# A two-block transformer on one core: six of the convolution's 31 taps become ScalarE products that DMAs add up, and its normalisation is put in another order

## The chip, the core and the metric

The kernel runs on one core of a Trainium2 chip. The metric is the device time of one execution in microseconds (us), as the median of several runs. An engine executes its own instructions strictly in the order of the program, so an instruction that waits holds up everything behind it on its engine.

## What is computed

Two transformer blocks in fp32 on 256 tokens of width 2048. The change lies in the first block, whose mixer has 16 attention heads (64 wide, three branches) beside a convolution branch with 1024 channels:

```
proj = rms_norm(x) @ w_in            # q | kv | gates | conv_in
a, gate = split(conv_in)
u = a * sigmoid(gate)                # 256 tokens x 1024 channels
u = causal_depthwise_conv(u, conv_w, conv_b)    # 31 taps
u = layer_norm(u, ln_g, ln_b)        # mean and variance over the 1024 channels
conv = silu(u)
x = x + concat([attn, conv]) @ w_out
```

After it come the block's feed-forward part and the second block, which the change does not touch.

## The kernel before, in words

The program is one list of weight items. An item is 128x1024 weights (512 KB): SyncE loads it (`raw`), ScalarE rounds it to `hi` (L281), VectorE subtracts to get `lo` (L282), and TensorE does 12 products of 128x512 with it (L164). Each of `hi` and `lo` has four buffers, so that ScalarE's cast for item n+3 can start when TensorE has finished item n-1. Eight items make a group of 512 columns. The order of the groups in the first block is the list `ORDER`: three quarters of the convolution's input (c0, c1, c2), gates, q0, cmp, c3 (the last quarter), win, slc, q1, and then the output projection, whose first part `oc` multiplies the convolution's eight blocks of 128 channels and needs no attention. Items are named here by group and place: q1.0 to q1.7, then oc.0 and so on.

Everything else is put between the items: after each half of an item the function `pump` lets each of three queues of small steps go on by a rate, the attention (`attn`), the convolution (`conv`, rates in `RATES`) and the urgent one (turning a group's result, and the like). When an item needs a convolution block that is not there, `Acts.get` runs the convolution's steps until it is.

A quarter q of the convolution has 256 channels in a 128x512 tile (two blocks side by side). One step of the queue is one tap: two VectorE instructions (L526) that multiply the shifted input `u` by a column and add to `y`; tap 30 is a ScalarE instruction with the bias (L523). When all four quarters are done, `conv_norm` goes on step by step: `mean` (TensorE with a matrix of 1/1024, over eight blocks), `center` for each quarter (VectorE subtracts, ScalarE squares), `var` (TensorE), `rs` and `rs2` (one over the root of the variance, spread over the partitions as `lnr`), then for each quarter `scale` for two halves (VectorE times `lnr`, ScalarE tanh, ScalarE gain and bias), `silu` (VectorE, then a ScalarE cast `sh`) and `low` (VectorE, `sl`). `sh` and `sl` are what oc multiplies.

At the end of q1 its result is taken from PSUM by two ScalarE copies (`e`, L428); TensorE turns `e` (L391) after oc.0, ahead of oc.1.

Of the kernel before, what the change touches and what calls it, by code (L numbers as in the profile page):

```python
# [19 lines left out]
AF = mybir.ActivationFunctionType  # L20
ALU = mybir.AluOpType
# [4 lines left out]
P = 128  # L26
T = 256
# [7 lines left out]
NU = 63  # L35
AHEAD = 3
NRAW = 4
LN_DVE = 0
ORDER = ["c0", "c1", "c2", "g", "q0", "cmp", "c3", "win", "slc", "q1", "oc", "oa", "ob"]
RATES = {"c1": {"conv": 1}, "win": {"attn": 0.25}, "q1": {"attn": 0.34, "conv": 1.5},  # L40
         "oc": {"attn": 0.5, "conv": 2}, "oa": {"attn": 1}}


# [31 lines left out]
class Pipe:  # L75


    def __init__(self):
        self.q = deque()
        self.later = []  # L80
# [26 lines left out]
class Acts:  # L107


    def __init__(self, pipe):  # L110
        self.d = {}
        self.pipe = pipe if callable(pipe) else lambda kt: pipe

    def get(self, kt):
        while kt not in self.d:
            assert self.pipe(kt).busy()
            self.pipe(kt).step()
        return self.d[kt]

    def put(self, kt, hi, lo):  # L120
# [3 lines left out]
def body(tc, A, out, stop=None, dbg=None):  # L124
# [18 lines left out]
    act, dve, pe, pool_e = nc.scalar, nc.vector, nc.tensor, nc.gpsimd  # L143
# [3 lines left out]
    def nm(s):  # L147
        cnt[0] += 1
        return f"{s}{cnt[0]}"

    def U(s="u", dt=F32):
        return big.tile([P, 512], dt, name=nm(s), tag="U", bufs=NU)

    def two(t):
        return t.rearrange("p (a b) -> p a b", a=2)

    def small(s="s"):
        return sml.tile([P, 16], F32, name=nm(s), tag="sm")

    def bank(s="bg"):  # L160
        return psB.tile([P, 512], F32, name=nm(s), tag="bg")

    def mm(o, l, r, start=False, stop=False):
        pe.matmul(o, l, r, start=start, stop=stop, skip_group_check=True)  # L164
# [138 lines left out]
    avg = keep.tile([P, P], F32, name="avg")  # L303
# [32 lines left out]
    def col(name, i):  # L336
        c = offs[name] + i
        return cols[:, c:c + 1]
# [73 lines left out]
    def turn_plain(dst, src, c0, c1=None):  # L412
        act.copy(dst, turn4(src, c0, c1))
# [72 lines left out]
    w_in = w2d("w_in")  # L486


    us, ys = {}, {}
    conv, attn = Pipe(), Pipe()  # L490
    mixT = Acts(lambda kt: conv if kt >= 8 else attn)

    def conv_in(q):

        def post(acc):
            s, u = U("sig"), U("ut")
            uu = [two(u)[:, 0], two(u)[:, 1]]
            for t in range(2):
                act.activation(two(s)[:, t], acc[t][:, :T], AF.Sigmoid, scale=rstd[:, t:t + 1])
                dve.scalar_tensor_tensor(uu[t], acc[t][:, T:], rstd[:, t:t + 1], two(s)[:, t],  # L500
                                         op0=ALU.mult, op1=ALU.mult)

            def f():
                us[q], ys[q] = U("u"), U("y")
                turn_plain(us[q], uu, 0)
                for k in range(30, -1, -1):
                    conv.push(lambda k=k: conv_tap(q, k))
                if q == 3:
                    conv_norm()
            urgent.push(None)  # L510
            urgent.push(f)
        return post

    def conv_group(q):
        group(w_in, None, 512, allk, xT, conv_in(q), parts=[(3632 + q * T, T), (2608 + q * T, T)])

    def conv_tap(q, k):
        u2, y2 = two(us[q]), two(ys[q])
        for kk in range(2):
            f = 2 * q + kk  # L520
            w = col("conv_w", k * 8 + f)
            if k == 30:
                act.activation(y2[:, kk], u2[:, kk], AF.Identity, scale=w, bias=col("conv_b", f))  # L523
            else:
                s = 30 - k
                dve.scalar_tensor_tensor(y2[:, kk, s:], u2[:, kk, :T - s], w, y2[:, kk, s:],  # L526
                                         op0=ALU.mult, op1=ALU.add)

    def conv_norm():
        st = {}  # L530

        def mean():
            b = st["m"] = bank("mean")
            for f in range(8):
                mm(b[:, :T], avg, two(ys[f // 2])[:, f % 2], start=f == 0, stop=f == 7)

        def center(q):
            mb = st["m"][:, :T].unsqueeze(1).broadcast_to([P, 2, T])
            dve.tensor_tensor(two(ys[q]), two(ys[q]), mb, op=ALU.subtract)
            s = st[q] = U("sqc")  # L540
            act.activation(s, ys[q], AF.Square)

        def var():

            b = st["v"] = bank("var")
            for t in range(2):
                for f in range(8):
                    mm(b[:, t:t + 1], two(st[f // 2])[:, f % 2, t * P:(t + 1) * P], avg[:, 0:1],
                       start=f == t == 0, stop=f == 7)

        half_gb = keep.tile([P, 16], F32, name="half_gb")

        def rs():
            c = offs["conv_ln_g"]
            dve.tensor_scalar(half_gb, cols[:, c:c + 16], 0.5, None, op0=ALU.mult)
            v = small("lnv")
            dve.tensor_scalar(v[:, :2], st.pop("v")[:, :2], EPS, None, op0=ALU.add)
            newton_rstd(v[:, 2:4], v[:, :2], 2)
            d = st["d"] = U("lnd")
            for t in range(2):  # L560
                dve.tensor_scalar(d[:, t * P:(t + 1) * P], ident, v[:, 2 + t:3 + t], 1024.0,
                                  op0=ALU.mult, op1=ALU.mult)

        def rs2():

            b = bank("lnr")
            mm(b[:, :T], avg, st.pop("d")[:, :T], start=True, stop=True)
            r = U("lnr")
            act.copy(r[:, :T], b[:, :T])
            st["r"] = r[:, :T]  # L570

        def scale(q, kk):
            y = two(ys[q])[:, kk]
            dve.tensor_tensor(y, y, st["r"], op=ALU.mult)

            if kk == 0:
                st[q] = U("th")
            f = 2 * q + kk
            g, b = half_gb[:, f:f + 1], half_gb[:, 8 + f:9 + f]
            act.activation(two(st[q])[:, kk], y, AF.Tanh, scale=g, bias=b)  # L580
            if LN_DVE:
                dve.tensor_scalar(y, y, g, b, op0=ALU.mult, op1=ALU.add)
            else:
                act.activation(y, y, AF.Identity, scale=g, bias=b)

        def silu(q):
            y = ys[q]
            dve.scalar_tensor_tensor(y, st.pop(q), 1.0, y, op0=ALU.add, op1=ALU.mult)
            hi = st["hi", q] = U("sh", F32R)
            act.copy(hi, y)  # L590

        def low(q):
            hi, lo = st["hi", q], U("sl", F32R)
            dve.tensor_tensor(lo, ys[q], hi.bitcast(F32), op=ALU.subtract)  # L594
            for kk in range(2):
                mixT.put(8 + 2 * q + kk, two(hi)[:, kk], two(lo)[:, kk])

        for f in (mean, None):
            conv.push(f)
        for q in range(4):  # L600
            conv.push(lambda q=q: center(q))
        for f in (None, var, rs, None, rs2):
            conv.push(f)
        for q in range(4):
            conv.push(lambda q=q: scale(q, 0))
            conv.push(lambda q=q: scale(q, 1), None, lambda q=q: silu(q), None, lambda q=q: low(q))

# [39 lines left out]
    def post_cmp(acc):  # L647
        e = take(acc, rstd)
        st = {}
# [22 lines left out]
        def hidden(i):  # L672
            def f():
                b = st[("b", i)] = bank("hid")
                o = b[0:64, :60]
                for lp in range(16):
                    e_, m = divmod(lp, 8)
                    xv = st[i][e_].rearrange("p (h n b) -> p h n b", h=4, b=8)
                    w = w1t[i][e_].rearrange("p (l c) -> p l c", l=8)[:, m]
                    mm(o, w, xv[:, :, e_:e_ + 15, m], start=lp == 0, stop=lp == 15)  # L680
            return f

        def silu():
            hk_ = st["hk"] = U("hidk")
            act.activation(hk_[0:64, :60], st.pop(("b", 0))[0:64, :60], AF.Silu)
            hv = st["hv"] = U("hidv")
            pool_e.memset(hv[0:64], 0.0)
            h4 = hv.rearrange("p (h g n) -> p h g n", h=4, g=4)
            src = st.pop(("b", 1))[0:64, :60].rearrange("p (h n) -> p h n", h=4)
            for g in range(4):  # L690
                act.activation(h4[0:64, :, g, 0:15], src, AF.Silu)
# [27 lines left out]
        for f in (gather(0), gather(1), hidden(0), hidden(1), silu, None, outk, outv):  # L719
            urgent.push(f)  # L720
# [261 lines left out]
    for name in ORDER:  # L982
        i0 = len(items)

        def bef(name=name):
            rates.update(RATES.get(name, {}))
            if name == "q0":
                load_M(0)
# [616 lines left out]
```

## Time and profile before

| what | value |
|---|---|
| median of 3 runs | 2831.16 us (2830.11 to 2831.34) |
| the profiled execution, its own time | 2829.45 us |
| its span, first to last instruction | 2827.5 us |
| TensorE (PE) busy | 2793.4 us, 99% |
| VectorE (DVE) busy | 1631.5 us, 58% |
| ScalarE (ACT) busy | 1423.6 us, 50% |
| GpSimd (POOL) busy | 36.6 us, 1% |
| mean granted TensorE clock | 0.996 |

Times in rows are microseconds from the start of the span; a duration runs from the start to the end of one instruction, and instructions of one engine overlap a little, so that the next one can start before the one in front has ended. Idle time in square brackets is that of the engine ahead of the row, with what ended it.

### The profile page before, as it was taken

The numbers are of one execution on the slowest core, as the hardware profiler recorded it, in microseconds if no ns is written. First come the engines' busy times: TensorE is split into PE (matmuls) and PEld (weight loads), VectorE is DVE, ScalarE is ACT, GpSimd is POOL, SyncE is SP. The second block draws the span as 40 slices with busy tenths as digits, with TensorE's granted clock in tenths as the row PEclk, the third lists the DMA queues.
The fourth block names the chain that finished last, engine by engine and source line by source line (L and its number), as shares of the span: only waits on it lengthen the run. The fifth ranks groups of instructions, "written<-read, shape, count | busy, mean of one in ns | idle before, by whom it ended". The sixth has DMA issues, their size and how long they took to land.

```text
span 2827.5 us, 34906 instructions
## 1 busy us (share of the span) xinstructions
PE 2793.4 (99%) x13031; PEld 2314.5 (82%) x13031; DVE 1631.5 (58%) x2472; ACT 1423.6 (50%) x2072; POOL 36.6 (1%) x73
## 2 busy tenths in 40 slices
PE   8998999999999999999999999999999999999998
PEld 7886778888888888889888888888888888888887
DVE  6887765656666554565554545555555455454444
ACT  5456565555555444566544555554454444444443
POOL 1200000000000000000000000000000000000000
PEclk9999999999999999999999999999999999999999
DMA  7853345666556666654566555665566666666664
GB/s 232 236 165 119 116 136 184 187 186 186 180 180 195 198 197 193 179 173 129 170 197 193 172 165 173 179 197 187 183 189 187 192 187 192 187 187 196 197 197 160
DMA packets 279579, 513.01 MB, mean 181 GB/s; under 512 B 21223, under 2 KB 46739, under 8 KB 279409
## 3 DMA queue, kind: packets, MB, share of 16 engines
q1 hardware_dynamic: 272256, 502.86, 58.4%
q0 software_dynamic: 4624, 7.13, 0.9%
q8 instruction: 102, 1.67, 0.2%
q10 hardware_dynamic: 2528, 0.79, 0.1%
q14 instruction: 69, 0.56, 0.1%
HBM read 505.45 MB, written 5.24 MB: 181 GB/s over the span
## 4 chain that ended last, share of the span: by engine, by line
PE 96%; DVE 1%; ACT 1%; issue 1%; DMA 0%; SPq 0%; DVEq 0%; ACTq 0%
PE acc L164 90%; PE tr L391 2%; PE ms L164 1%; PE o L164 0%; DMA raw<-in_w_in 0%; PE ds L164 0%; PE mo L164 0%; PE do L164 0%; DVE lo L282 0%; ACT hi L281 0%; ACT p L802 0%; PE hid L164 0%; PE s L164 0%; PE pt L807 0%; DVE y L526 0%
## 5 line engine op out<-in xcount | busy, mean ns | idle before, releaser
L282 DVE TENSOR_TENSOR lo<-raw,hi 128x1024 fp32r<-128x1024 f32 (+3 forms) x956 | 1153.3, 1211 | 1013.7 <-ACT hi L281 993.1
L281 ACT CAST hi<-raw 128x1024 fp32r<-128x1024 f32 (+3 forms) x956 | 989.8, 1040 | 879.3 <-PE acc L164 821.2
L164 PE MATMUL acc<-hi,xh 128*128 128x512 f32 (+2 forms) x3200 | 1261.2, 394 | 2.8 <-ACT xh L405 2.8
L164 PE MATMUL acc<-hi,xl 128*128 128x512 f32 (+2 forms) x3200 | 1241.8, 388 | 0.5 <-DVE xl L407 0.5
L164 PE MATMUL acc<-lo,xh 128*128 128x512 f32 (+2 forms) x3200 | 1240.0, 388 | 0.0
L164 PEld LDWEIGHTS acc<-hi,xl 128*128 128x128 f32 x3200 | 601.7, 188 | 123.7 <-DVE xl L407 1.0
L164 PEld LDWEIGHTS acc<-hi,xh 128*128 128x128 f32 x3200 | 602.2, 188 | 118.4 <-ACT xh L405 3.0
L164 PEld LDWEIGHTS acc<-lo,xh 128*128 128x128 f32 x3200 | 602.8, 188 | 115.9 <-DVE lo L282 0.5
L164 PE MATMUL acc<-hi,sh 128*128 128x512 f32 x480 | 192.1, 400 | 10.7 <-ACT sh L590 10.7
L164 PE MATMUL acc<-hi,sl 128*128 128x512 f32 x480 | 187.7, 391 | 0.0
L164 PE MATMUL acc<-lo,sh 128*128 128x512 f32 x480 | 187.6, 391 | 0.0
L164 PEld LDWEIGHTS acc<-hi,sh 128*128 128x128 f32 x480 | 90.6, 189 | 29.4 <-ACT sh L590 11.1
L164 PEld LDWEIGHTS acc<-hi,sl 128*128 128x128 f32 x480 | 90.5, 188 | 19.6 <-DVE sl L594 0.2
L164 PEld LDWEIGHTS acc<-lo,sh 128*128 128x128 f32 x480 | 90.7, 189 | 17.6
L526 DVE SCALAR_TENSOR_TENSOR y<-u,cols,y 128x255 f32<-128x255 f32 (+14 forms) x240 | 96.3, 464 | 0.0
L1043 DVE SCALAR_TENSOR_TENSOR yf<-tr,cols,yf 128x254 f32<-128x254 f32 (+1 forms) x176 | 72.6, 475 | 29.3 <-ACT yf L1038 29.3
L1038 ACT ACTIVATE yf<-tr,cols 128x256 f32<-128x256 f32 x88 | 44.8, 560 | 33.7 <-PE tr L391 33.7
L164 PE MATMUL acc<-hi,ymh 128*128 128x512 f32 x128 | 49.8, 389 | 0.0
L164 PE MATMUL acc<-lo,ymh 128*128 128x512 f32 x128 | 49.8, 389 | 0.0
L164 PE MATMUL acc<-hi,yml 128*128 128x512 f32 x128 | 49.8, 389 | 0.0
L428 ACT ACTIVATE e<-acc,rstd 128x512 f32<-128x512 f32 x54 | 37.0, 690 | 25.2 <-PE acc L164 25.2
L434 ACT ACTIVATE junk<-xs 128x512 f32<-128x512 f32 x48 | 30.0, 629 | 35.8 <-DVE xs L442 14.3
(314 smaller groups left out, 1373.5 us busy)
## 6 DMA issues: line engine op xcount, KB each, us to landing
raw<-in_w_in SPq DMA_DIRECT2D x216, 512.0 KB, 3.7
raw<-in_w_up SPq DMA_DIRECT2D x176, 512.0 KB, 3.8
raw<-in_w_down SPq DMA_DIRECT2D x88, 512.0 KB, 4.4
raw<-in_w_ffn_gate SPq DMA_DIRECT2D x88, 512.0 KB, 4.3
raw<-in_w_ffn_up SPq DMA_DIRECT2D x88, 512.0 KB, 3.8
raw<-in_w_ffn_down SPq DMA_DIRECT2D x88, 512.0 KB, 4.3
raw<-in_w_out SPq DMA_DIRECT2D x64, 512.0 KB, 3.7
raw<-in_w_in SPq DMA_DIRECT2D x64, 256.0 KB, 3.4
```

Of the source, the lines that this page charges most:

```text
L164: pe.matmul(o, l, r, start=start, stop=stop, skip_group_check=True)
L281: act.copy(it.hi[:, c], it.raw[:, c])
L282: dve.tensor_tensor(it.lo[:, c], it.raw[:, c], it.hi[:, c].bitcast(F32), op=ALU.subtract)
L391: pe.transpose(b[:, kk * T + t * P: kk * T + (t + 1) * P], src[t][:, c:c + P], ident)
L428: act.activation(u[:, :n], acc[t][:, :n], AF.Copy, scale=scale[:, t:t + 1])
L434: act.activation(j[:, :n], src, AF.Square, accum_out=acc)
L526: dve.scalar_tensor_tensor(y2[:, kk, s:], u2[:, kk, :T - s], w, y2[:, kk, s:], op0=ALU.mult, op1=ALU.add)
L1038: act.activation(y2[:, kk], t2[:, kk], AF.Identity, scale=c(2), bias=col("ffn_conv_b", f))
L1043: dve.scalar_tensor_tensor(y2[:, kk, s:], t2[:, kk, :T - s], col("ffn_conv_w", k * 88 + f), y2[:, kk, s:], op0=ALU.mult, op1=ALU.add)
```

## The change

Taps with shifts 3, 6, 9, 12, 15 and 18 leave VectorE: ScalarE multiplies (`conv_product`), and a DMA issued from GpSimd adds the product to the tile `y` of tap 30 (`conv_gather`). The other taps add up in a new tile `z`, and `conv_join` adds the two. A running sum of the quarters (`csum`) and of the squares is kept by VectorE, so that `mean` and `var` need a quarter of the products. The centring goes two quarters to a step, gain and bias go from ScalarE to VectorE (`LN_DVE`), a quarter has 25 or 26 steps in place of 31, the rate in c1 is 0.88, and each of the two `hidden` steps of cmp runs three convolution steps. A wait for a convolution block would also step the attention.

```diff
-LN_DVE = 0
+LN_DVE = 1
-RATES = {"c1": {"conv": 1}, "win": {"attn": 0.25}, "q1": {"attn": 0.34, "conv": 1.5},
+RATES = {"c1": {"conv": 0.88}, "win": {"attn": 0.25}, "q1": {"attn": 0.34, "conv": 1.5},
...
             self.pipe(kt).step()
+            if self.other and kt not in self.d:
+                self.other(kt)
...
-                for k in range(30, -1, -1):
-                    conv.push(lambda k=k: conv_tap(q, k))
+                conv.push(lambda: (conv_tap(q, 30), conv_tap(q, 29)))
+                for s in range(2, 31):
+                    if s % 3 == 0 and s <= 18:
+                        continue
+                    if s % 3 == 2 and s < 18:
+                        conv.push(lambda s=s: (conv_tap(q, 30 - s), conv_product(q, s + 1)),
+                                  lambda s=s: conv_gather(q, s + 1))
+                    else:
+                        conv.push(lambda s=s: conv_tap(q, 30 - s))
+                conv.push(lambda: conv_join(q))
+                if q:
+                    conv.push(lambda: conv_sum(q))
...
+    def conv_product(q, s):
+        z = prods[q, s] = U("pr")
+        for kk in range(2):
+            act.activation(two(z)[:, kk, s:], two(us[q])[:, kk, :T - s], AF.Copy,
+                           scale=col("conv_w", (30 - s) * 8 + 2 * q + kk))
+
+    def conv_gather(q, s):
+        pool_e.dma_start(two(ys[q])[:, :, s:], two(prods.pop((q, s)))[:, :, s:],
+                         accum_op=ALU.add)
+
+    def conv_join(q):
+        y, z = two(ys[q])[:, :, 1:], two(zs[q])[:, :, 1:]
+        dve.tensor_tensor(y, y, z, op=ALU.add)
...
+    def conv_sum(q):
+        if q == 1:
+            csum.append(U("csum"))
+        s = csum[0]
+        dve.tensor_tensor(s, ys[q], s if q > 1 else ys[0], op=ALU.add)
...
-            for f in range(8):
-                mm(b[:, :T], avg, two(ys[f // 2])[:, f % 2], start=f == 0, stop=f == 7)
+            s = two(csum.pop())
+            for kk in range(2):
+                mm(b[:, :T], avg, s[:, kk], start=kk == 0, stop=kk == 1)
...
             act.activation(s, ys[q], AF.Square)
+            if q:
+                p = st[q - 1]
+                dve.tensor_tensor(s, s, p, op=ALU.add)
...
-        for q in range(4):
-            conv.push(lambda q=q: center(q))
+        for q in (0, 2):
+            conv.push(lambda q=q: (center(q), center(q + 1)))
         for f in (None, var, rs, None, rs2):
             conv.push(f)
-        for q in range(4):
+        conv.push(lambda: (scale(0, 0), scale(0, 1)))
+        conv.push(lambda: silu(0))
+        conv.push(lambda: low(0))
+        for q in range(1, 4):
```

How the order moves is seen at three places. First VectorE, around the centring (`mean` is TensorE's result, `sqc` a square from ScalarE, `rg` the attention's normalisation). Before:

```order
L539 TENSOR_TENSOR y_509<-y_509,mean_2203 128x512
L282 TENSOR_TENSOR lo_2222<-raw_2056,hi_2221 128x1024
L539 TENSOR_TENSOR y_715<-y_715,mean_2203 128x512
L850 RECIPROCAL rg_2254<-sm_2185 128x4
...
L539 TENSOR_TENSOR y_929<-y_929,mean_2203 128x512
L539 TENSOR_TENSOR y_1671<-y_1671,mean_2203 128x512
```

In the changed kernel the join and the sum stand ahead of the mean, and VectorE adds squares between the centrings:

```order
L285 TENSOR_TENSOR lo_2100<-raw_2011,hi_2099 128x1024
L544 TENSOR_TENSOR y_1734<-y_1734,z_1735 128x2x255
L568 TENSOR_TENSOR csum_1312<-y_1734,csum_1312 128x512
...
L581 TENSOR_TENSOR y_509<-y_509,mean_2121 128x512
L581 TENSOR_TENSOR y_738<-y_738,mean_2121 128x512
L586 TENSOR_TENSOR sqc_2178<-sqc_2178,sqc_2175 128x512
L581 TENSOR_TENSOR y_954<-y_954,mean_2121 128x512
L586 TENSOR_TENSOR sqc_2188<-sqc_2188,sqc_2178 128x512
L581 TENSOR_TENSOR y_1734<-y_1734,mean_2121 128x512
L586 TENSOR_TENSOR sqc_2192<-sqc_2192,sqc_2188 128x512
```

So each addition stands between two centrings and reads a square that ScalarE makes of the centring in front.

Second TensorE, where the mean's products stand: before behind four score products (`s`) after q1.4's first half,

```order
L164 MATMUL s_2181<-kx_89,q_1168 128x143
L164 MATMUL s_2182<-kx_89,q_1168 128x143
L164 MATMUL mean_2203<-y_509,avg 128x256 x2
L164 MATMUL mean_2203<-y_715,avg 128x256 x2
L164 MATMUL mean_2203<-y_929,avg 128x256 x2
L164 MATMUL mean_2203<-y_1671,avg 128x256 x2
```

and in the changed kernel at the end of q1.0, ahead of the turning of slc's keys (`kt`):

```order
L167 MATMUL acc_2106<-lo_2030,xh_128 128x512
L167 MATMUL acc_2106<-hi_2029,xl_129 128x512
L167 MATMUL mean_2121<-csum_1312,avg 128x256 x2
L394 MATMUL tr_2124<-ident,kt_2094 128x128 x4
L167 MATMUL acc_2105<-hi_2051,xh_187 128x512
```

The mean has moved ahead by three and a half items; `var` now stands after the first half of q1.2 and `lnr` after the first half of q1.3 (before: after q1.6 and after q1.7).

Third ScalarE, where it takes q1's result (`e`). Before it stands behind the first tanh (`th`) of quarter 0:

```order
L569 COPY lnr_2357<-lnr_2355 128x256
L580 ACTIVATE th_2360<-y_509,half_gb 128x256
L584 ACTIVATE y_509<-y_509,half_gb 128x256
L428 ACTIVATE e_2363<-acc_2023,rsq 128x512
L428 ACTIVATE e_2365<-acc_2024,rsq 128x512
```

Now it stands behind the last cast of quarter 3:

```order
L636 CAST sh_2377<-y_738 128x512
L284 CAST hi_2379<-raw_2199 128x1024
L626 ACTIVATE th_2392<-y_1734,half_gb 128x256 x2
L636 CAST sh_2401<-y_954 128x512
L284 CAST hi_2409<-raw_2252 128x1024
...
L636 CAST sh_2442<-y_1734 128x512
L431 ACTIVATE e_2452<-acc_2105,rsq 128x512
L431 ACTIVATE e_2454<-acc_2106,rsq 128x512
```

All steps of the normalisation have moved in front of `e`, since all of them are put out by the end of q1.7.

## Rows read from the trace of the kernel before

**Rows 1.** The page's part 1: busy time, share of span, instructions.
```profile
PE 2793.4 (99%) x13031; PEld 2314.5 (82%) x13031; DVE 1631.5 (58%) x2472; ACT 1423.6 (50%) x2072; POOL 36.6 (1%) x73
```
**Rows 2.** Waits of PE, 70 to 520 us: total, times, longest.
```profile
PE acc L164 <- ACT sh L590: 10.7, 1, 10.7
PE mean L164 <- DVE y L526: 3.1, 1, 3.1
```
**Rows 3.** Timeline of PE, 215 to 270 us: start, duration, line, tiles.
```profile
215.23 0.60 PE L391 MATMUL tr<-ident,kt 128*128 128x128 f32 x4
...
227.34 2.86 PE L164 MATMUL mean<-y,avg 128*128 128x256 f32 x12
233.30 1.13 PE L164 MATMUL mean<-y,avg 128*128 128x256 f32 x4 [3.11 <-DVE y L526]
...
243.41 3.62 PE L164 MATMUL var<-avg,sqc 128*128 128x1 f32 x32
...
262.08 0.79 PE L164 MATMUL acc<-hi,sh 128*128 128x512 f32 x1 [10.67 <-ACT sh L590]
...
268.49 0.48 PE L164 MATMUL acc<-hi,sh 128*128 128x512 f32 x1
```
**Rows 4.** Windows: length, busy (count) of PE, PEld, DVE, ACT, POOL, clock, DMA.
```profile
260.00:280.00 20.00, 17.92 (x94) 13.58 (x94) 13.68 (x40) 15.42 (x32) 1.82 (x3) 0.86 0.26 77
```
**Rows 5.** Timeline of DVE, 219 to 249 us.
```profile
219.24 1.23 DVE L282 TENSOR_TENSOR lo<-raw,hi 128x1024 fp32r<-128x1024 f32 x1
...
221.85 2.32 DVE L526 SCALAR_TENSOR_TENSOR y<-u,cols,y 128x234 f32<-128x234 f32 x6
...
225.22 0.29 DVE L945 SCALAR_TENSOR_TENSOR lj<-lq 128x128 f32<-128x128 f32 x1
...
227.60 0.35 DVE L855 TENSOR_SCALAR p<-p,rg 128x256 f32<-128x256 f32 x1
...
228.72 1.56 DVE L526 SCALAR_TENSOR_TENSOR y<-u,cols,y 128x230 f32<-128x230 f32 x4
...
247.07 0.16 DVE L557 TENSOR_SCALAR lnv<-var 128x2 f32<-128x2 f32 x1 [0.80 <-PE var L164]
...
248.49 0.48 DVE L561 TENSOR_SCALAR lnd<-ident,lnv 128x128 f32<-128x128 f32 x2
```
**Rows 6.** Timeline of ACT, 209 to 256 us.
```profile
209.98 1.06 ACT L281 CAST hi<-raw 128x1024 fp32r<-128x1024 f32 x1 [1.67 <-PE acc L164]
...
213.47 1.06 ACT L281 CAST hi<-raw 128x1024 fp32r<-128x1024 f32 x1
...
222.62 1.03 ACT L281 CAST hi<-raw 128x1024 fp32r<-128x1024 f32 x1
...
248.43 1.28 ACT L802 ACT_TABLE_LOAD   x1
...
254.24 1.25 ACT L428 ACTIVATE e<-acc,rsq 128x512 f32<-128x512 f32 x2
```
**Rows 7.** Instructions on tile y: shortest/median/longest in ns, first and last start.
```profile
L574 DVE TENSOR_TENSOR y<-y,lnr x8: 418/419/426, 252.6 to 263.6; 128x256 f32<-128x256 f32 x8
L580 ACT ACTIVATE th<-y,half_gb x8: 584/594/600, 253.1 to 265.9; 128x256 f32<-128x256 f32 x8
...
L539 DVE TENSOR_TENSOR y<-y,mean x4: 674/678/690, 236.1 to 242.7; 128x512 f32<-128x512 f32 x4
L541 ACT ACTIVATE sqc<-y x4: 615/630/633, 236.9 to 243.4; 128x512 f32<-128x512 f32 x4
...
L590 ACT CAST sh<-y x4: 602/602/622, 261.4 to 269.0; 128x512 fp32r<-128x512 f32 x4
```
**Rows 8.** Landing of POOL's loads of M (256 KB), in us.
```profile
DMA to landing us min/median/max: 3.1/4.2/15.0
```
**Rows 9.** DMA issues: tiles, queue, count, KB each, median us to landing.
```profile
gsc<-gm POOLq DMA_DIRECT2D x4, 768.0 KB, 14.4
...
w<-in_cmp_w POOLq DMA_DIRECT2D x2, 16.0 KB, 12.2
```

More of the change, by code (lines that the diff above doesn't have):

```diff
@@ L112, in __init__ @@
         self.pipe = pipe if callable(pipe) else lambda kt: pipe
+        self.other = None
     def get(self, kt):
@@ L486, in body @@
     w_in = w2d("w_in")
-    us, ys = {}, {}
+    us, ys, zs, prods = {}, {}, {}, {}
     conv, attn = Pipe(), Pipe()
     mixT = Acts(lambda kt: conv if kt >= 8 else attn)
+    mixT.other = lambda kt: (attn if kt >= 8 else conv).step()
     def conv_in(q):
@@ L503, in f @@
             def f():
-                us[q], ys[q] = U("u"), U("y")
+                us[q], ys[q], zs[q] = U("u"), U("y"), U("z")
                 turn_plain(us[q], uu, 0)
-                for k in range(30, -1, -1):
-                    conv.push(lambda k=k: conv_tap(q, k))
+                conv.push(lambda: (conv_tap(q, 30), conv_tap(q, 29)))
[10 more added lines that the diff above has]
+                    conv.push(lambda: conv_sum(q))
                 if q == 3:
@@ L515, in conv_group @@
         group(w_in, None, 512, allk, xT, conv_in(q), parts=[(3632 + q * T, T), (2608 + q * T, T)])
+    def conv_product(q, s):
[9 more added lines that the diff above has]
+        dve.tensor_tensor(y, y, z, op=ALU.add)
     def conv_tap(q, k):
-        u2, y2 = two(us[q]), two(ys[q])
+        u2, y2 = two(us[q]), two(ys[q] if k == 30 else zs[q])
         for kk in range(2):
@@ L525, in conv_tap @@
                 s = 30 - k
+                if s == 1:
+                    dve.tensor_scalar(y2[:, kk, s:], u2[:, kk, :T - s], w, None, op0=ALU.mult)
+                    continue
                 dve.scalar_tensor_tensor(y2[:, kk, s:], u2[:, kk, :T - s], w, y2[:, kk, s:],
                                          op0=ALU.mult, op1=ALU.add)
+    csum = []
+    def conv_sum(q):
[3 more added lines that the diff above has]
+        dve.tensor_tensor(s, ys[q], s if q > 1 else ys[0], op=ALU.add)
     def conv_norm():
@@ L541, in center @@
             act.activation(s, ys[q], AF.Square)
+            if q:
+                p = st[q - 1]
+                dve.tensor_tensor(s, s, p, op=ALU.add)
         def var():
             b = st["v"] = bank("var")
+            s = two(st[3])
             for t in range(2):
-                for f in range(8):
-                    mm(b[:, t:t + 1], two(st[f // 2])[:, f % 2, t * P:(t + 1) * P], avg[:, 0:1],
-                       start=f == t == 0, stop=f == 7)
+                for kk in range(2):
+                    mm(b[:, t:t + 1], s[:, kk, t * P:(t + 1) * P], avg[:, 0:1],
+                       start=kk == t == 0, stop=kk == 1)
         half_gb = keep.tile([P, 16], F32, name="half_gb")
@@ L680, in f @@
                     mm(o, w, xv[:, :, e_:e_ + 15, m], start=lp == 0, stop=lp == 15)
+                for _ in range(3):
+                    conv.step()
             return f
```

## The prediction

> **What bounds the kernel.** I read the busy table first: TensorE is at work for 2793.4 of 2827.5 us [rows 1], so a change can gain only where TensorE waits or loses its clock. The list of TensorE's waits shows two long ones in the convolution's end: 3.1 us ahead of the mean and 10.7 us ahead of the first product of oc [rows 2]. The timeline puts them: products of the mean run from 227.34, stop for the last tap and go on at 233.30; then nothing runs until 262.08, when ScalarE's first `sh` is there; oc.1 starts at 268.49 [rows 3]. Over the 20 us that begin 2.1 ahead of the end of the long wait the granted clock is 0.86 [rows 4]: 5.6 us at the lower of the two levels (1.2 GHz in place of 2.4, so 0.5 of full). 2.1 of them are waiting; the other 3.5 are work, of which half, 1.7 us, is lost. A better order could so give back about 13.8 of waits, 1.7 or a little more of clock, and the TensorE work removed (next). Everything after oc.1 is the same program, so the prediction is one number: when does oc.1 start, and at what clock?
>
> **What is removed and added.** Twelve products of the mean took 2.86 us, 0.24 each; twelve of sixteen go: 2.9. Of 32 variance products in 3.62, 24 go: 2.6 [rows 3]. Together 5.5 us less for TensorE, worth that only where TensorE is not held for something else. VectorE loses 48 taps at 0.37 (six take 2.32 [rows 5]), 18 us, and gets four joins, three sums, three additions of squares (a subtraction of that shape takes 0.68 [rows 7]) and eight gain-and-bias instructions (0.35 [rows 5]), 10 us. ScalarE gets 48 products; nearest is the tanh of that shape, 0.59 [rows 7], 28 us, and loses eight others. Until q1.0 both are hidden: in every item of 2.72 us ScalarE sits idle for 1.67 until TensorE frees a buffer [rows 6], and the split is three items ahead, 8 us; lag beyond that would cost TensorE one for one. Stepping the attention in a wait for a convolution block costs and gives nothing: all blocks are put out by the end of q1.7, so no such wait comes up; the steps in cmp and the rates only set when taps are put out.
>
> **From q1.0 to the variance.** TensorE reaches the end of q1.0 as before, at 215.23 [rows 3]. There the mean now stands. ScalarE's cast runs at 213.47 to 214.53 [rows 6], VectorE's split ends 1.14 later (219.24 to 220.38 [rows 5], where the scores begin), at 215.7; join and sum, 0.68 each [rows 7], end at 217.1. Term one: TensorE waits 1.9. The mean's four products take 0.95, and the turning of the keys starts at 218.1, 2.9 later than before. Key copies, cast, split and the scores' eight instructions follow as before: there they ended at 221.85 on VectorE and 222.62 on ScalarE [rows 5, 6], now at 224.7 and 225.5. Then centring 0, 1 (0.68 each [rows 7], less their overlap, to 226.0); squares 0, 1 behind the exponentials (0.63 each less overlap, to 226.65); addition, 227.4; centring 2 overlaps a little, 228.0; square, 228.65; addition, 229.4; centring 3, 230.0; square, 230.65; addition, 231.4. Each alternates between the engines, since the addition stands ahead of the next centring. TensorE has by then done one item and a half and the scores, and is at the variance at 223.8. Term two: it waits 7.6.
>
> **To `lnr`.** Behind the variance VectorE has a split (its cast ends at 231.6: 232.8), the lambda instructions and an attention normalisation (225.22 to 228.72 less two taps of 0.37: 2.76), and the root's chain of small instructions (247.07 to 248.97: 1.9) [rows 5]: 237.6. TensorE is there after the variance (0.9), one item and up to 1.7 of lost clock, at 235 to 237. Term three: about 1.6. `lnr` and its copy take it to 238.6.
>
> **To `e`.** From here TensorE has five and a half items of 2.72 to the end of oc.0, and attention products that I estimate at 4 to 5 (of the 6.4 from 262.08 to 268.49, 2.7 are oc.0 and 1.7 clock, 2 such products): it is done at about 258. The chain of VectorE and ScalarE is longer. For each half of a quarter: multiply 0.42, tanh 0.59 [rows 7], gain and bias 0.35 [rows 5], each waiting for the one in front (the last one overwrites what tanh reads, and the next multiply stands behind it): about 1.3, overlaps taken off, eight times 10.5. Into it the order puts a table load of 1.28 [rows 6] ahead of the first tanh, four splits, each with a cast that stands behind a tanh or an `sh` (1.05 + 1.14 less some overlap, 8.5), two sets of scores with exponentials (1.5 and 1.2), a normalisation with the compressed branch (1.8), four `silu` and four `sh` (0.68 and 0.60, nearly all in line: 5), and `sl` (0.6 each, two in line). Walked through in the order of both engines it reads: `sl` of quarter 0 done at 247.4, `silu` 1 at 257.3, `sl` 1 at 263.5, `sh` 2 at 264.8, `sh` 3 at 270.1, and the two `e` copies (1.25 [rows 6]) at 271.2. The turning of `e` stands ahead of oc.1 on TensorE. Term four: TensorE waits from 258 to 271.2, 13 us. One rule weighs on a single item here. The trace has a table load at 1.28 [rows 6]. The Trainium skill (ScalarE: Activation LUTs, "Table sets: the hidden batching unit") puts one load at about 2.7 us and exp and tanh in one set; by its price `e` would come 1.4 later, by the row it stands as above.
>
> **The sum.** oc.1 starts 0.4 after `e`, at 271.6, against 268.49: 3.1 later. In before the loss of clock behind the long wait was already paid by then, now it comes after: 1.7 more. 4.8 us. Put the other way: waits 24 in place of 13.8, against 5.5 of TensorE work less, all of it swallowed. The walk has some forty instructions in line, and each may be 0.1 off: 4 us to both sides.
>
> **The gathers.** The trace has no adding DMA. Nearest are POOL's loads of M, as large (256 KB): 3.1 to 15, median 4.2 [rows 8]; the long ones stood behind a write to `gsc`, 14.4, as did a 16 KB load that took 12.2 [rows 9], so POOL's queue is served in order. Six gathers of a quarter add to one tile, so each waits for the one in front. I take 4 to 5 us each. Quarter 3 has 13 items, 36 us, from its first gather to its join, room for 6.1 each. Quarter 1 is the tight one: its second gather stands behind a `gsc` write, its fourth behind the issue of the cmp weights. I estimate 28 us for the write (14.4), some ten DMAs issued at about one us and what lands behind them, and three more gathers in line: 40 us at 4 each, 43 at 5, 46 at 6. From the first gather to the join there are 12.5 items, 35 us, and the split three items ahead lets VectorE be held for 6 more, 41, before TensorE stands. So 0 to 2 us, 5 at 6 us each; a gain is excluded, since nothing waits for the gathers' work in before. I take 0, since the median is nearest to 4. The Trainium skill (DMA: Bandwidth & Descriptors, "Anatomy of one DMA — SWDGE (gpsimd) path") fits such a DMA with 2.0 us plus its bytes at 436 GB/s: an estimate of 2.6 for 256 KB, less than any row here, and by it no join waits.
>
> **Forecast.** 2829.45 (the profiled execution's own time) + 4.8 = 2834.3; the runs' median stands 1.7 above that execution: 2836.0. That is 0.17% up, just inside the 0.2% (5.7 us) that a measurement of this kernel can tell from no change.
>
> **Rivals.**
> - *Faster* (the chain behind `lnr` is shorter than I walk it). ScalarE was busy 15.4 and VectorE 13.7 of 20 us in such a stretch [rows 4], so if neighbours overlap more than the order seems to let them, `e` comes early. It decides below 260.8, ten of the chain's 32.6 us; at 258 oc.1 would start at once, without a lost clock: 10.5 less than before, 2821. Against it: every tanh is read by its follower on the other engine. 14%.
> - *The gathers hold VectorE* at the joins: at 6 us each 5 more (2841), at 7 eight at quarter 1 and 5 at quarter 3 (2849). For it: an adding DMA reads its destination too, and the weights' stream keeps the DMA engines busy. Against it: the median 4.2 was under that stream. 26%.
> - *Nothing left over*: the same waits, but the walk is 3 to 8 us too long, so that oc.1 starts by up to 5 us earlier than before or as then, and the later loss of clock eats it: 2828 to 2833. 15%.
> - My forecast, 2833 to 2840: 45%, three fifths of it inside the 0.2%.
>
> Faster so 14%, the same 15 + 27 = 42%, slower 26 + 18 = 44%. The range leaves out the faster case and the far end of the gathers: 2827 to 2847.
>
> **What would show it.** Right: the mean waits about 2 us for the sum, the variance 6 to 9 for the last square, the longest wait is 11 to 15 at the turning of `e` (for ScalarE's `e`) and none is left at `sh`; the granted clock falls there. Wrong: TensorE waits in 100 to 200 us (a join held by a gather; then gathers land in over 5), or `e` is taken before 262.

## The result: 0.7% slower, and the profile after

The changed kernel takes 2852.52 us (median of 6 runs, 2843.86 to 2855.08), the kernel before 2830.87 beside it: ratio 1.0073, 95% interval 1.0061 to 1.0085. The forecast was 2836.0 in a range of 2827 to 2847. The time lies above the range, near the rival "the gathers hold VectorE" at its far end (2849).

The page's part 1 of the changed kernel: TensorE is busy for 7 us more in a span 22.8 us longer, although it has 36 products fewer: a product at the lower clock counts as busy for longer (0.63 us in place of 0.39 in the timelines).

```profile
PE 2800.7 (98%) x12995; PEld 2318.1 (81%) x12995; DVE 1622.9 (57%) x2442; ACT 1436.9 (50%) x2112; POOL 65.2 (2%) x97
```

TensorE's waits in the changed kernel from 60 to 320 us (what waited for what, total, times, longest). In before the two long ones were 10.7 and 3.1 [rows 2]; here there are seven, 29.7 us.

```profile
PE mean L167 <- DVE csum L568: 8.1, 1, 8.1
PE var L167 <- DVE sqc L586: 6.4, 1, 6.4
PE pt L860 <- DVE mx L849: 6.1, 1, 6.1
PE acc L167 <- DVE lo L285: 2.9, 1, 2.9
PE vc L167 <- POOL vcmp L764: 2.1, 1, 2.1
PE tr L394 <- ACT e L431: 2.1, 1, 2.1
PE s L167 <- ACT pts L863: 2.0, 1, 2.0
```

Where the time went is seen best by putting the first product of an item in one timeline beside the same product in the other (starts in us):

| product | before | changed | later by |
|---|---|---|---|
| c3.0 | 135.78 | 135.31 | -0.5 |
| c3.1 | 138.86 | 143.20 | 4.3 |
| c3.7 | 163.90 | 168.25 | 4.4 |
| win.1 | 170.74 | 180.37 | 9.6 |
| q1.0 | 212.50 | 222.16 | 9.7 |
| q1.1 | 215.58 | 235.69 | 20.1 |
| q1.4 | 224.99 | 257.35 | 32.4 |
| oc.0 | 262.08 | 275.10 | 13.0 |
| oc.1 | 268.49 | 289.81 | 21.3 |
| oc.2 | 272.68 | 295.38 | 22.7 |
| end of the span | 2827.5 | 2850.3 | 22.8 |

Three steps of 4.8, 5.3 and 10.4 us lie ahead of the centring, at places where before had no wait (between c3.0 and c3.1, c3.7 and win.1, q1.0 and q1.1). From q1.1 to oc.2 the difference goes up and down, as each kernel waits at places of its own, but only 2.6 are left of that.

All three steps lead back to GpSimd's queue; of the third, 2.9 us belong to the new order (first run below). The queue's timeline in the changed kernel (start, duration of the issue, in brackets the idle time ahead and what ended it):

```profile
90.97 1.59 POOL L831 DMA_DIRECT2D gsc<-gm  x1
95.03 1.24 POOL L539 DMA_DIRECT2D y<-pr  x1 [2.46 <-ACT hi L284]
108.97 1.19 POOL L539 DMA_DIRECT2D y<-pr  x1 [12.70 <-DMA y<-pr]
...
115.11 1.21 POOL L539 DMA_DIRECT2D y<-pr  x1 [0.25 <-issue]
125.25 1.20 POOL L539 DMA_DIRECT2D y<-pr  x1 [8.93 <-DMA y<-pr]
131.30 1.17 POOL L539 DMA_DIRECT2D y<-pr  x1 [4.85 <-issue]
132.30 1.30 POOL L831 DMA_DIRECT2D gsc<-gm  x1
133.44 1.41 POOL L539 DMA_DIRECT2D y<-pr  x1
149.94 1.18 POOL L539 DMA_DIRECT2D y<-pr  x1 [15.09 <-DMA y<-pr]
...
171.00 1.18 POOL L539 DMA_DIRECT2D y<-pr  x1 [3.27 <-DMA y<-pr]
171.71 1.01 POOL L740 MEMSET hidv<- 64x512 f32 x1
...
191.05 1.21 POOL L539 DMA_DIRECT2D y<-pr  x1 [16.34 <-ACT pr L535]
196.68 1.18 POOL L539 DMA_DIRECT2D y<-pr  x1 [4.42 <-DMA y<-pr]
205.07 1.18 POOL L539 DMA_DIRECT2D y<-pr  x1 [7.21 <-DMA y<-pr]
211.59 1.17 POOL L539 DMA_DIRECT2D y<-pr  x1 [5.34 <-DMA y<-pr]
217.69 1.19 POOL L539 DMA_DIRECT2D y<-pr  x1 [4.93 <-DMA y<-pr]
226.97 1.18 POOL L539 DMA_DIRECT2D y<-pr  x1 [8.09 <-DMA y<-pr]
```

Quarter 3's gathers follow one another at 7.2 us ((226.97 - 191.05) / 5), each held until the one in front has landed. The gathers behind a `gsc` write (95.03 and 133.44) keep their followers waiting for 12.7 and 15.1 us, the one behind the loads of the cmp weights (115.11) for 8.9. The memset of `hidv`, which the attention's cmp branch needs, stands behind all gathers of quarter 2.

Who was held by it: the joins of quarters 1 and 3 on VectorE, and ScalarE at `hidv`, in their timelines.

```profile
136.03 0.69 DVE L544 TENSOR_TENSOR y<-y,z 128x510 f32<-128x510 f32 x1 [5.23 <-DMA y<-pr]
...
231.63 0.69 DVE L544 TENSOR_TENSOR y<-y,z 128x510 f32<-128x510 f32 x1 [6.19 <-DMA y<-pr]
```

```profile
172.75 0.53 ACT L744 ACTIVATE hidv<-hid 64x60 f32<-64x60 f32 x4 [13.68 <-POOL hidv L740]
```

Behind a held join stand the splits, and TensorE waits for a `lo` (2.9) or for the sum (8.1). Each of the three steps is longer than the wait in it (2.9, 2.1 and 8.1); the third also holds the mean's four products, 1.9 us, which in before come later. The windows of the changed kernel around the three steps and around `e` (length, busy of PE, PEld, DVE, ACT, POOL, granted clock, DMA share):

```profile
133.00:143.00 10.00, 7.06 (x25) 5.33 (x25) 6.93 (x12) 4.81 (x8) 1.85 (x2) 0.83 0.82 168
170.00:181.00 11.00, 8.88 (x29) 7.12 (x28) 6.72 (x12) 8.15 (x21) 3.71 (x5) 0.69 0.55 133
225.00:250.00 25.00, 10.52 (x41) 8.16 (x40) 10.08 (x28) 9.70 (x19) 5.18 (x8) 0.70 0.49 106
270.00:295.00 25.00, 15.20 (x63) 11.10 (x63) 15.78 (x42) 13.36 (x27) 1.79 (x3) 0.73 0.34 104
```

So the wait of 2.1 us for `vcmp` made a step of 5.3: in that window the granted clock is 0.69, and products start 0.43 apart where they otherwise start 0.23 apart.

### The profile page after: what moved, and what is told of

It is laid out like the page before. It is cut to its first block, busy times and chain, and to the rows that moved or that the text cites. A ratio compares the mean times of both kernels' runs of the same rounds, so it can differ in the third digit from the quotient of the medians.

```text
span 2850.3 us, 34903 instructions
## 1 busy us (share of the span) xinstructions
PE 2800.7 (98%) x12995; PEld 2318.1 (81%) x12995; DVE 1622.9 (57%) x2442; ACT 1436.9 (50%) x2112; POOL 65.2 (2%) x97
## 4 chain that ended last, share of the span: by engine, by line
PE 91%; DMA 3%; DVE 3%; ACT 2%; issue 1%; SPq 0%; POOL 0%; DVEq 0%; ACTq 0%; POOLq 0%
PE acc L167 85%; PE tr L394 2%; DMA y<-pr 2%; DMA raw<-in_w_in 1%; DVE lo L285 1%; PE ms L167 1%; ACT hi L284 1%; PE o L167 0%; DVE z L558 0%; PE ds L167 0%; PE mo L167 0%; PE do L167 0%; ACT p L855 0%; PE s L167 0%; DMA M<-gsc 0%
## 5 line engine op out<-in xcount | busy, mean ns | idle before, releaser
L558 DVE SCALAR_TENSOR_TENSOR z<-u,cols,z 128x254 f32<-128x254 f32 (+22 forms) x184 | 73.7, 462 | 0.0
L437 ACT ACTIVATE junk<-xs 128x512 f32<-128x512 f32 x48 | 30.0, 630 | 35.9 <-DVE xs L445 14.3
```

The source lines that it names most:

```text
L437: act.activation(j[:, :n], src, AF.Square, accum_out=acc)
```

## The experiments

Theory A: the gathers cost the time, by holding the joins and by standing ahead of the memsets. Theory B: the normalisation's new order does. Later theories are named where they come up. Times are medians; the ratio is to the kernel before beside it.

**Without the gathers.**

```diff
 def conv_gather(q, s):
-    pool_e.dma_start(two(ys[q])[:, :, s:], two(prods.pop((q, s)))[:, :, s:],
-                     accum_op=ALU.add)
+    prods.pop((q, s))
```

> The changed kernel with its 24 adding DMAs left out (ScalarE still makes the six products of a quarter, nothing adds them, so six taps are missing from the convolution). Theory A, the gathers cost the time (VectorE held at the joins of quarters 1 and 3, the memsets of cmp queued behind quarter 2's gathers): the three delays of 4.8, 5.3 and some 8 us ahead of the centring go, TensorE waits about 2 us at the mean, and the kernel takes 2833 to 2838 us, as the walk of the prediction has it. Theory B, the new order of the normalisation costs it: the early delays only replace waits that come later, and the kernel stays at 2846 us or more.

2834.73 us, ratio 1.0015 (1.0005 to 1.0024): 17.8 less than the changed kernel (16.5 between the spans of the two profiled executions). Theory A holds, and theory B is left with the 4 us above before. TensorE's waits in this run, 60 to 320 us:

```profile
PE var L167 <- DVE sqc L585: 6.4, 1, 6.4
PE pt L859 <- DVE mx L848: 6.1, 1, 6.1
PE tr L394 <- ACT e L431: 2.1, 1, 2.1
PE s L167 <- ACT pts L862: 2.0, 1, 2.0
PE mean L167 <- DVE csum L567: 1.8, 1, 1.8
```

The four waits of the normalisation are the same as with gathers, to 0.1 us; only those at `lo` and `vc` and 6.3 of the mean's are gone. The mean's wait and its products make q1.1 2.9 later here, the order's own share of the third step. oc.1 starts at 273.21, 4.7 later than in before.

**The memsets ahead.** The three memsets are issued in `load_cmp`, ahead of the cmp weights.

```diff
 def load_cmp():
+    pre["hv"], pre["v"] = U("hidv"), [U("vcmp"), U("vcmp")]
+    pool_e.memset(pre["hv"][0:64], 0.0)
+    for v in pre["v"]:
+        pool_e.memset(v, 0.0)
```

> The changed kernel with the three memsets of cmp (hidv, two vcmp) put ahead of the cmp weights in GpSimd's queue. Theory A: the 2.1 us wait of TensorE at vc and the 3 us of lower clock around it go, and the join of quarter 3 comes no later: 2846 to 2849 us. If that wait is only part of the time until quarter 3's gathers have landed, the mean waits longer by the same amount and the time stays at 2850 to 2854 us.

2845.11 us (2839.31 to 2847.39, 4 runs), ratio 1.0049 (1.0034 to 1.0064): 7.4 less by the medians, more than the step at `vc` alone. The profiled execution is the fastest of the four. In it the first gather of quarter 3 is issued 10.0 us earlier than in the changed kernel, though q1.0 starts only 6.3 earlier (215.86), the six follow one another at 6.5 us, and the mean waits 2.2 in place of 8.1:

```profile
181.07 1.21 POOL L539 DMA_DIRECT2D y<-pr  x1 [9.19 <-ACT pr L535]
...
213.75 1.18 POOL L539 DMA_DIRECT2D y<-pr  x1 [4.68 <-DMA y<-pr]
```

```profile
PE mean L167 <- DVE csum L568: 2.2, 1, 2.2
```

The delay of ScalarE at `hidv` so also makes quarter 3's products and gathers late: an estimate from these two executions is that 3.7 us (10.0 - 6.3) of the third step are the memset's, not the gathers' period. How much of the 7.4 that is in the others can't be told from one profile.

**The old normalisation.** `conv_norm` of before, gathers and joins kept.

> The changed kernel with the mean, the centring, the variance and the scaling of before (no running sums, gain and bias on ScalarE, one quarter to a step), gathers and joins kept. In the changed kernel 56.7 us lie between the start of the mean's products and oc.1; in before 35.2 us between the start of the mean's last products and oc.1. If the chain behind the mean is what sets oc.1 (theory C), the old chain behind a join that ends at 232 gives oc.1 at 268 to 272 us and 2829 to 2834 us in all, although the gathers still delay the joins. If the delays ahead of the mean simply add up (theory A alone), it stays at 2845 us or more.

2847.42 us, ratio 1.0053 (1.0036 to 1.0070). Theory C is refuted: q1.1 starts at 236.33, 20.8 later than in before, since the mean stands at the end of q1.0 here too, and this is not given back. oc.1 comes 17.3 later than in before, not 21.3. By the medians the order is worth 5 us, but this interval and the changed kernel's overlap; the run without gathers is the better measure of it.

**Two chains.** Shifts 12 and 18 are added to the product of 6, which VectorE adds at the join; three gathers in line in place of six.

```diff
...
+        y, z = two(ys[q])[:, :, 6:], two(prods.pop((q, 6)))[:, :, 6:]
+        dve.tensor_tensor(y, y, z, op=ALU.add)
```

> The changed kernel with each quarter's gathers in two chains: shifts 3, 9 and 15 are added to y, shifts 12 and 18 to the product of shift 6, which VectorE adds at the join (five adding DMAs in place of six, at most three in line, four additions of 0.69 us more on VectorE). If the length of the chain of gathers holds the joins, the waits at the joins of quarters 1 and 3 go, and with them 8 to 14 us: 2838 to 2844 us. If it is the throughput of the queue or of the DMA engines, the joins come hardly earlier: 2848 to 2854 us.

2841.43 us, ratio 1.0035 (1.0022 to 1.0048): 11.1 less than the changed kernel, with 20 gathers in place of 24. Four gathers of 24 fewer would give 3 of the 17.8; it is mostly the length of the line that counts.

**Two chains, the memsets ahead, and a lower rate in q1.**

```diff
-... "q1": {"attn": 0.34, "conv": 1.5} ...
+... "q1": {"attn": 0.34, "conv": 1.0} ...
```

> The changed kernel with two chains of gathers, the memsets of cmp ahead of its weights, and the convolution's rate in q1 at 1 step a half item in place of 1.5, so that ScalarE's taking of q1's result stands behind two casts of the normalisation fewer (behind sh of quarter 0 only, not of quarter 3) and the mean and the variance stand an item or more later. With the gathers out of the way 4.7 us are left over from the normalisation's order (waits 1.8 at the mean, 6.4 at the variance, 6.1 and 2.1 in front of the turning of e, 2.0 at a score). If the order in front of e and the early variance make these waits (theory C), at least the 8.2 ahead of e and part of the 6.4 go: 2820 to 2829 us, faster than before. If the chain of VectorE and ScalarE is simply as long (theory D), the wait moves to the first product with sh: 2832 to 2838 us.

2841.11 us, ratio 1.0037 (1.0024 to 1.0051). No gain over the run with two chains (2841.43), and above the ranges of both theories. Theory C is out; theory D had it right that the waits would move (that for `mx` ahead of `e` is gone, and others stand at `sh`, `sl` and `lnr`), but not the price, and three things were changed at once. Of its waits:

```profile
PE var L167 <- DVE sqc L595: 7.6, 1, 7.6
PE acc L167 <- ACT sh L645: 6.9, 2, 5.7
...
PE acc L167 <- DVE sl L649: 3.1, 1, 3.1
PE lnr L167 <- DVE lnd L616: 2.2, 1, 2.2
```

**Copies in place of additions.** Only `accum_op` is left out.

> The changed kernel with the 24 adding DMAs made plain copies of the product to the same place (y is overwritten in place of added to, so the convolution is not the reference's). If reading the destination and adding is what makes a gather land in 5.6 us at the median and not in 4.2 like a load of the same size, the landing falls to about 4.2, the chain of quarter 3 ends some 8 us earlier, and the time falls to 2836 to 2842 us. If the DMA engines' other traffic and the wait of each for the one in front set it, the landing stays above 5 and the time at 2848 to 2855 us.

2840.00 us, ratio 1.0028 (1.0016 to 1.0040): 12.5 less. The landing of the 24 DMAs, changed kernel first, then this run:

```profile
DMA to landing us min/median/max: 3.8/5.6/15.9
```

```profile
DMA to landing us min/median/max: 2.5/3.8/14.3
```

An addition lands 1.8 us later than a copy of the same shape, and its issue takes GpSimd 1.19 us at the median and not 0.71. Without the adding 12.5 of the 17.8 us that the gathers cost are gone. In quarter 3 the medians are 5.8 and 3.3. The longest is a DMA behind a `gsc` write in both.

**All taps on VectorE, and half the gathers.** First `conv_tap(q, 29 - s)` in place of product and gather; second, the same for shifts 6, 12 and 18 only, with the memsets ahead.

> The changed kernel with the six taps of a quarter back on VectorE (no products, no gathers; joins, sums and the new normalisation kept). VectorE gets 48 instructions of 0.4 us back, 19 us over the four quarters. If it has room for them until q1.0, as it is busy 127 of 160 us there in the changed kernel, the time is that of the kernel without gathers or up to 4 us above it: 2833 to 2839 us. If VectorE becomes the bound in quarter 3, the mean waits 5 us or more: 2840 to 2846 us.

> Half the gathers: shifts 3, 9 and 15 by ScalarE and DMA, 6, 12 and 18 as taps on VectorE, the memsets of cmp ahead of its weights, everything else as in the changed kernel. If three gathers in line of 5 to 8 us are hidden behind the other taps, no join waits, and it is at the time without gathers: 2833 to 2838 us. If the gathers cost by their number, half of the 18 us is left: 2840 to 2845 us.

2834.81 us (1.0014, 1.0005 to 1.0023) and 2834.20 us (1.0012, 1.0003 to 1.0021): both the time without gathers. VectorE had room for all taps, so that taking them off was worth nothing here; three gathers in line of 4.0 to 15.1 us (median 5.7) are hidden, with the memsets out of their way. The kernel with three gathers still stands 3 us above before, and the next runs ask why.

**The old normalisation at its old place.** On the run with three gathers:

```diff
-        for f in (mean, None):
+        for f in (None,) * 9 + (mean, None):
```

> Three gathers a quarter and the early memsets (as in the run that had them), with the mean, centring, variance and scaling of before, and the mean put off by nine empty steps, two and a half items of weights, to about where it stood in before. The convolution is complete at about 217 and not at 233 us, so that no product of the mean should wait. If the chain behind the mean sets oc.1 (theory D), it starts about 4 us earlier than in before (all sixteen mean products end by 230 in place of 234.4) and the wait at the first sh falls from 10.7 to about 6: 2823 to 2828 us. If the earlier convolution frees nothing, since the attention's steps fill VectorE and ScalarE: 2829 to 2834 us.

2830.46 us, ratio 0.9999 (0.9990 to 1.0009): level with before, in the second of the two ranges. The convolution is complete ahead of the mean, which does not wait, and oc.0 starts at 256.07, 6.0 earlier than in before; but a new wait at `sl` takes it back, and oc.1 starts at 268.43, as in before, where theory D had it 4 earlier. TensorE's waits, and why `sl` is late, on VectorE:

```profile
PE acc L167 <- ACT sh L632: 5.0, 1, 5.0
PE acc L167 <- DVE sl L636: 4.9, 1, 4.9
```

```profile
253.29 0.69 DVE L630 SCALAR_TENSOR_TENSOR y<-th,y 128x512 f32<-128x512 f32 x1 [1.28 <-ACT y L626]
258.14 1.22 DVE L285 TENSOR_TENSOR lo<-raw,hi 128x1024 fp32r<-128x1024 f32 x1 [4.16 <-ACT hi L284]
...
261.47 0.69 DVE L636 TENSOR_TENSOR sl<-y,sh 128x512 fp32r<-128x512 f32 x1
```

`sl` of quarter 0 is queued behind a split, whose cast stands behind `sh` and `e` on ScalarE.

**The attention put off, the steps interleaved, and both apart.** Interleaved means that a quarter's two multiplications, two tanh and two gain-and-bias stand in this order, and all four centrings ahead of the additions of squares; some empty steps between the normalisation's steps move too.

```diff
-... "q1": {"attn": 0.34, ...}, "oc": {"attn": 0.5, ...} ...
+... "q1": {"attn": 0, ...}, "oc": {"attn": 0.67, ...} ...
```

> Three gathers and early memsets with the changed kernel's normalisation; the attention's rate is 0 in q1 and 0.67 in oc (before 0.34 and 0.5), so that no scores and exponentials stand between the steps of the normalisation. In the changed kernel some 12 us of VectorE and ScalarE work of two sets of scores, a third ahead of e and two normalisations stand in that chain. If they are what makes it 55 us long from the mean to oc.1 (theory E): 2820 to 2827 us. If the steps of the normalisation themselves are too long for the TensorE work beside them, or the attention is late at oa instead: 2830 to 2836 us.

> As the run with the attention put off, and the steps of the normalisation written so that neither engine waits for each one's result: four centrings, then the three additions of squares; both multiplications of a quarter, both tanh, both gain-and-bias. By the changed kernel's rows VectorE waited 0.7 three times at the additions and 0.67 to 0.8 eight times at the scaling, some 8 us. On top of theory E: 2816 to 2823 us. If the attention was no cause, this alone gives 2828 to 2832 us.

> The same order of the normalisation's instructions, with the attention's rates of the changed kernel (three gathers, early memsets). If waits of VectorE and ScalarE for each other are what is left over of the 4 us: 2826 to 2831 us. If the attention's steps between them set the length: 2831 to 2835 us.

2838.23 us (1.0027, 1.0016 to 1.0037), 2833.23 (1.0011, 1.0002 to 1.0020) and 2832.00 (1.0001, 0.9992 to 1.0011). The first two lie above both of their ranges, the third in its upper one. Theory E is refuted as a gain: with the attention put off oc.1 starts 1.7 earlier than in before, and interleaved too 6.8 earlier, but at the end of oc they are 8.7 and 3.7 behind it: the attention's work put off comes there, and TensorE waits 4.7 for its `pcts`. The interleaving alone takes 2.2 off the 2834.2 by the medians; the two intervals overlap, so that this is not settled.

**Old normalisation at its old place, interleaved, with `sl` right behind `silu`.** Against the run with the old normalisation at its old place, gain and bias also move from ScalarE to VectorE. The second run has all taps on VectorE.

```diff
-            conv.push(lambda q=q: scale(q, 0))
-            conv.push(lambda q=q: scale(q, 1), None, lambda q=q: silu(q), None, lambda q=q: low(q))
+            conv.push(lambda q=q: scale(q), lambda q=q: silu(q), lambda q=q: low(q))
+            conv.push(None)
```

> As the run with three gathers, early memsets and the old normalisation put off by nine empty steps, but the scaling of a quarter in one step (both multiplications, both tanh, both gain-and-bias on VectorE), silu in the next and sl right behind it, so that sl of quarter 0 stands ahead of the split that waits for ScalarE's cast behind e. In the run before TensorE waited 5.0 us at the first sh and 4.9 at the first sl. If these two queues take the gain back (theory F), the wait at sl goes and that at sh falls by the ScalarE work taken out in front of it (three gain-and-bias instructions of 0.6 and one tanh pair less): 2820 to 2827 us, faster than both kernels. If the chain is bound elsewhere, the wait moves to the turning of e or the next sh: 2828 to 2832 us.

> The same with all 30 taps of a quarter behind the first on VectorE (no products, no gathers). If VectorE has room, as the run with all taps on it showed for the changed kernel's order, it takes the same time as with three gathers, within 2 us. If the relief of VectorE is worth anything, it is 3 us or more slower.

2825.57 us (11 runs), ratio 0.9982 (0.9973 to 0.9991), and 2827.17 us, 0.9987 (0.9978 to 0.9996). Both beat both kernels, with intervals wholly below 1. The first lies in theory F's range, the second within the 2 us of it that were expected, and the waits went the theory's way: that at `sl` from 4.9 to 1.4, that at `sh` from 5.0 to 4.0, while a new one of 3.1 stands at the turning of `e`. The first one's waits at `sh` and `sl`:

```profile
PE acc L167 <- ACT sh L633: 4.0, 1, 4.0
...
PE acc L167 <- DVE sl L637: 1.4, 2, 0.8
```

The order of a handful of instructions behind `lnr`, with eight of them moved to VectorE, gains 4.9 us over the run with the old order at the same place (2830.46; the two intervals just touch). Which of the three changes (the place of `sl`, the interleaving, the move to VectorE) gives how much was not taken apart. Whether the three gathers a quarter are worth the 1.6 us between the two is not settled, since the intervals overlap.

## Why the prediction was wrong, step by step

- **Removed and added, until q1.0: the bounds held, one item was missed.** VectorE had room both ways. But "until q1.0 both are hidden" left out what else stands in GpSimd's queue: the memsets behind quarter 2's gathers, a step of 5.3 us. The timeline of GpSimd shows them there; the prediction went along the joins alone.
- **The gathers: the step that failed.** "I take 0, since the median is nearest to 4" priced a gather by POOL's loads of M [rows 8]. The gathers landed in 5.6 at the median, since an addition takes 1.8 longer than a copy, and followed one another at 7.2 us in quarter 3. The places were right: quarter 1 behind the `gsc` write and the cmp weights, which cost 4.8 (5 was the price at 6 us each), and quarter 3, where the step of 10.4 less the 2.9 of the run without gathers is 7.5 (5 was the price at 7; an estimated 3.7 of the 7.5 is the late start behind `hidv`, which the prediction did not see). 4.8 + 5.3 + 7.5 = 17.6, against 17.8 by the medians and 16.5 by the spans with the gathers left out. The Trainium skill (DMA: Bandwidth & Descriptors, "Anatomy of one DMA — SWDGE (gpsimd) path") gives 2.6 as an estimate for 256 KB; the traces do not agree at the median, with 3.8 for the copies and 5.6 for the additions; only the fastest copy, 2.5, does.
- **From q1.0 to the variance.** Without gathers the mean waits 1.8 (1.9 forecast) and the variance 6.4 (7.6). Right.
- **To `lnr` and to `e`.** The walk can be followed in the run without gathers:

```profile
231.00 0.69 DVE L585 TENSOR_TENSOR sqc<-sqc,sqc 128x512 f32<-128x512 f32 x1 [0.70 <-ACT sqc L582]
```

```profile
238.81 0.73 PE L167 MATMUL lnr<-lnd,avg 128*128 128x256 f32 x2
```

```profile
271.34 1.26 ACT L431 ACTIVATE e<-acc,rsq 128x512 f32<-128x512 f32 x2
```

  The last addition ends at 231.7 (231.4 forecast) and `e` at 272.6 (271.2), so the chain of VectorE and ScalarE was walked nearly right. The 1.4 came in at `lnr`: there TensorE, walked to 235 to 237, came last, at 238.8, without the wait of 1.6. Its granted clock was 0.80 from 225 to 250 us; the walk had allowed up to 1.7 us of lost clock. TensorE so came later to `e` too, and the 13 us there were 10.2 in three waits, 2.0, 6.1 and 2.1. The longest is not for `e` but for an attention maximum (`mx`), which is queued on VectorE behind a split that waits for a cast behind an `sh` on ScalarE (in the changed kernel at 283.85, 282.78 and 282.25). None was left at `sh`, as forecast. oc.1 was walked to 271.6 and came at 273.2.
- **The sum.** 4.8 without the gathers; the run that leaves them out is 3.8 above before by the medians (2834.73 against 2830.89) and 6.3 by the spans, 4.7 until oc.1 and 1.6 of lost clock behind it (1.7 forecast). The waits were 18.4 in all, not 24; TensorE lost to its clock (0.82 from 217 to 273 us) what it waited less, so the waits alone were a poor measure of the time. The forecast of 2836 was that kernel's time, not the changed one's.
- **The rivals.** "The gathers hold VectorE" was given 26% and was what happened at the joins (4.8, and 7.5 less the late start's share). Its far end (2849) took 8 and 5 there, 13 in all, where 12.3 came; the 5.3 at the memsets stood in no rival, and they are why the time lies above it. "Faster" was refuted: even without gathers `e` ends at 272.6, not below 260.8. What would have shown it wrong was named: a wait in 100 to 200 us, and gathers landing in over 5.

## What to carry to other kernels

A chain of DMAs that each wait for the one in front is priced by its whole period (7.2 us here, not a load's 4.2), and everything else queued on the issuing engine, a small memset too, is part of the price. Taking work off an engine gains nothing where that engine was not what the waiting engine waited for: all 24 taps could go back to VectorE at no cost (2834.8 against 2834.7 with them left out). Where two engines work in turn, look for the one instruction that stands behind a wait it doesn't need; `sl` ahead of a split, the scaling interleaved, and gain and bias on VectorE together made the only two versions here that are faster than before.

## What was not expected of the hardware

- An adding DMA of 238 to 253 KB landed in 5.6 us at the median, a plain one of the same shape in 3.8; the issue took 1.19 and 0.71 us.
- Gathers issued next behind a 768 KB write to `gsc` landed in 13.4 and 15.9 us, as copies in 14.3 and 10.4 (the last issued 5.6 us after the write): there it is the place behind the write, not the adding.
- A wait of TensorE of 2 to 3 us cost 4.8 and 5.3 in all, at a granted clock of 0.83 and 0.69 over the windows around it; two such waits were dearer than their length in the list of waits says.
